# Two modulation vectors of layer 0 computed on VectorE instead of TensorE

## The chip, the cores and the metric

The kernel runs on one core of a Trainium2 chip. The metric is the device time of one execution in microseconds, and lower is better. The kernel computes in float32. TensorE multiplies matrices, VectorE (DVE) and ScalarE (ACT) and GpSimd (POOL) work elementwise, and SyncE (SP) issues the transfers from the main memory (HBM) into the on-chip memory (SBUF). Each engine runs its own instructions strictly in the order in which they stand in its stream, and waits for other engines through semaphores.

## The reference

Two blocks of two layers each, on a sequence of 256 tokens, a context of 256 tokens and a width D = 1024. The first block has a differential attention layer (layer 0, 8 heads of two 64-wide halves) and a neighbourhood attention layer, both with a feed-forward part; the second block has two hybrid layers. What the change touches is the modulation of layer 0:

```python
silu_c, silu_cc = silu(c), silu(c_ctx)          # two vectors of 1024
sh1, sc1, g1, sh2, sc2, g2 = split(silu_c @ ada_w[i] + ada_b[i], 6)   # the same with silu_cc for the context
h = rmsnorm(x, norm_mix[i]) * (1 + sc1) + sh1
y, yc = diff_attention(h, hc, ...)              # 8 heads
x = x + g1 * y
h2 = rmsnorm(x, norm_ffn[i]) * (1 + sc2) + sh2  # needed only after the attention
x = x + g2 * conv_ffn(h2, ...)
```

A vector such as sc2 has 1024 entries, held as 8 columns of 128, each for two conditionings (token and context). Each column is a product of a 1024 x 128 block of weights with two vectors.

## The kernel before, in words

A float32 product is made of three TensorE products of a high and a low part (mm3, L332, L335, L336). The weights come by DMA into a tile "raw" (128 x 2048, 1 MB, three buffers in turn for everybody), ScalarE rounds them to the high part "whi" (L311) and VectorE forms the low part "wlo" = raw - whi (L312), each in pieces of 128 x 1024.

Layer 0 starts with norms and projections of v, and then goes through eight heads. For each head, proj makes q and k (24 products of 512 columns each for q and for k), which ScalarE and VectorE turn into qhi, qlo, khi, klo (L1108, L1110, L1112) after the rotary part (L1129 to L1132, of which L1130 on POOL). diff_head then forms scores on TensorE (L1122), maxima on VectorE (L1149), exponentials on ScalarE (L1151), the difference of two softmaxes on POOL and VectorE (L1157, L1158), transposes (L1163) and the product with v (L1169). At a head's end, the output is normed: squares on ScalarE (L1174), their sum "oss" (L1176 to L1178), the scaled output "p" on VectorE (L1179), four transposes of it on TensorE (L1184, called the head's end below) and the split into ohi and olo (L1185, L1186). After heads 6 and 7 the products with wo begin, whose results are added to the residual tile xT (L883).

Modulation of layer 0 on TensorE comes in 20 "pieces" (ada_piece): each loads 1 MB of weights (L368), runs 8 products of 256 columns on a quarter of the array (L384), copies on ScalarE (L393), transposes twice on TensorE (L399) and sums on VectorE (L405, L408, and L416 for a scale). A piece gives two columns. Eight pieces (shift and scale of the attention's norm) come ahead of the attention; twelve ("fill": gate, and shift and scale of the feed-forward norm) stand in the heads, by the row (2,2,2,2,1,1,1,1) of numbers by head. Modulation of the other layers is made later on VectorE in another way (L441): a row of weights times the broadcast silu(c) "cb", summed along the row by one instruction with an accumulator (scalar_tensor_tensor), which gives one column for one conditioning; cb is loaded and put through Silu at L428 and L429.

The residual tile xT holds 8 rows of 512 columns per partition. In the attention its first two rows are scratch for q and k, and they are loaded again (L907) in head 6.

A scheduler sets the order of the instructions on each engine; buffers set when a transfer may start.

Of the kernel before, what the change touches and what calls it, by code (L numbers as in the profile page):

```python
# [11 lines left out]
AF = mybir.ActivationFunctionType  # L12
ALU = mybir.AluOpType
# [3 lines left out]
P = 128  # L17
D = 1024
KC = 8
# [6 lines left out]
NFH = NF // 2  # L26
HORD = [0, 2, 1, 3]

PIECES = [((0, k), (1, k)) for k in range(KC)] + [((2, k), (3, k)) for k in range(KC)]
PIECES += [((4, 2 * k), (4, 2 * k + 1)) for k in range(KC // 2)]  # L30
ADAV = [(0, 5, k) for k in range(KC)] + [(1, v, k) for v in (0, 1, 2, 3, 4, 5) for k in range(KC)]


# [117 lines left out]
def _layout(i):  # L151
    a = {}
# [10 lines left out]
        [np.stack([aw[0, :, :, v, k] for v, k in pc], axis=2).transpose(1, 0, 2, 3).reshape(P, KC * 256) for pc in PIECES]  # L163
    )
    a["adav"] = np.stack([aw[l, :, :, v, k].reshape(D, P).T for l, v, k in ADAV])
    a["cb"] = np.broadcast_to(c2.reshape(1, 2 * D), (P, 2 * D))
    wq = i["a_wqkv"][0]
    order = [x for h in range(8) for x in (h, 8 + h)]
# [59 lines left out]
class K:  # L228
# [191 lines left out]
    def ada_steps(self, pool, n, after):  # L420

        nc = self.nc
        if self.aq >= 2 * len(ADAV):
            return
        if self.acb[1:] != [pool]:
            cb = self.t(pool, [P, 2, D], "cb")
            nc.vector.tensor_copy(cb[:, 0, 0:1], after)
            nc.sync.dma_start(cb, self.i["cb"].rearrange("p (c k) -> p c k", c=2))  # L428
            nc.scalar.activation(cb, cb, AF.Silu)  # L429
            self.acb = [cb, pool]  # L430
        for _ in range(n):
            if self.aq >= 2 * len(ADAV):
                return
            e, c = divmod(self.aq, 2)
            self.aq += 1
            l, v, k = ADAV[e]
            if c == 0:
                self.araw = self.t(pool, [P, D], "araw", bufs=3)
                nc.sync.dma_start(self.araw, self.i["adav"][e])
            junk = self.t(pool, [P, D], "junk", mybir.dt.bfloat16)  # L440
            nc.vector.scalar_tensor_tensor(  # L441
                junk, self.araw, 1.0, self.acb[0][:, c, :], op0=ALU.mult, op1=ALU.mult,
                accum_out=self.ada[l][:, v, k, c : c + 1],
            )
            if self.aq % (2 * KC) == 0:
                self.ada_vector(e // KC)

    def ada_vector(self, g):

        nc = self.nc  # L450
        l, v, _ = ADAV[g * KC]
        ab = self.V("adab").rearrange("p (l v k) -> p l v k", l=DEPTH, v=6)[:, l, v, :]
        dst = self.ada[l][:, v, :, :]
        nc.vector.tensor_tensor(
            dst, dst, ab.rearrange("p (k o) -> p k o", o=1).to_broadcast([P, KC, 2]), op=ALU.add
        )
        if v in (1, 4):
            w = 0 if v == 1 else 1
            gn = self.V("nmix" if w == 0 else "nffn")[:, l * KC : l * KC + KC]
            nc.vector.scalar_tensor_tensor(  # L460
                self.nA[l][w], dst, 1.0, gn.rearrange("p (k o) -> p k o", o=1).to_broadcast([P, KC, 2]),
                op0=ALU.add, op1=ALU.mult,
            )
# [274 lines left out]
    def layer0(self):  # L738
        nc, i = self.nc, self.i
        with ExitStack() as cx:  # L740
# [156 lines left out]
            for h in range(8):  # L897
                q, k = nxt
                self.diff_head(hp, h, q, k, v, nlam, ohi, olo)
                if h < 7:  # L900
                    nxt = proj(h + 1)
                for _ in range((2,2,2,2,1,1,1,1)[h]):
                    self.ada_piece(fill.pop(0))
                if h == 6:
                    for hf in range(2):
                        c = slice(T * hf, T * hf + T)
                        nc.sync.dma_start(self.xT[:, 0:2, c], i["xin"][hf, :, 0:2, :])  # L907
                    wo_load(0, 1)
                    for m in (4, 5):
                        wo(0, m, (0, 1), self.acc)  # L910
# [846 lines left out]
```

## Time and profile before

| | us |
|---|---|
| runs of the kernel, median (lowest to highest of 3) | 1579.35 (1578.86 to 1582.08) |
| the profiled execution | 1579.73 |
| its span from the first to the last instruction | 1577.9 |
| TensorE (PE) busy in the span | 1548.6 (98%) |
| VectorE (DVE) busy | 1116.0 (71%) |
| ScalarE (ACT) busy | 770.1 (49%) |
| GpSimd (POOL) busy | 345.7 (22%) |
| layer-0 attention, about | 84 to 292 of the span |

Times in the profile are microseconds from the span's start. A busy share of an engine is an average: what a change is worth is read from the stretch in which it stands, and from which wait ends last there. "PEld" is TensorE's loading of weights, which runs beside its products. "PEclk" is the granted clock of TensorE as a share of full speed. A line of the code is given as L12.

### The profile page before, as it was taken

What the parts mean: (1) busy time and instruction counts of PE and PEld (TensorE: products, weight loads), DVE (VectorE), ACT (ScalarE), POOL (GpSimd) and SP (SyncE); (2) the same over time, 40 slices, a digit from 0 to 9 for tenths busy, and PEclk for the clock granted to TensorE, in tenths of its full rate; (3) what the DMA queues carried; (4) which work ended last, traced back from release to release, by engine and by line L of the source; (5) the groups of instructions that cost most, each with busy time, mean ns of one, the idle gap of its engine ahead of it and who ended that gap; (6) DMA issues with size and microseconds to landing.
All of it is one profiled execution on the core that took longest, in us unless ns stands there. A gap on an engine that the chain in (4) does not pass through costs nothing. (4 is left out here: it accounts for less than half of the span.)

```text
span 1577.9 us, 26663 instructions
## 1 busy us (share of the span) xinstructions
PE 1548.6 (98%) x10390; PEld 1354.7 (86%) x10390; DVE 1116.0 (71%) x2006; ACT 770.1 (49%) x1385; POOL 345.7 (22%) x418
## 2 busy tenths in 40 slices
PE   8999999999999999999999999999999999999998
PEld 6777777788888888888777899999899999899998
DVE  4556777678999999363554796778577667767665
ACT  4445554454322443343544684665554445555443
POOL 0012221321100111200111150123345214242222
PEclk9999999999999999999999999999999999999999
DMA  8523332335467654233221445547235555335552
GB/s 335 193 80 134 112 149 91 118 121 194 155 211 273 209 179 152 95 130 125 106 95 67 161 163 199 187 155 280 102 137 177 180 207 216 134 108 201 175 200 81
DMA packets 49373, 251.93 MB, mean 160 GB/s; under 512 B 5088, under 2 KB 8160, under 8 KB 31584
## 3 DMA queue, kind: packets, MB, share of 16 engines
q1 hardware_dynamic: 49248, 250.23, 44.4%
q8 instruction: 82, 1.34, 0.3%
q14 instruction: 43, 0.35, 0.1%
HBM read 249.16 MB, written 1.05 MB: 159 GB/s over the span
## 5 line engine op out<-in xcount | busy, mean ns | idle before, releaser
L311 ACT ACTIVATE whi<-raw 128x1024 fp32r<-128x1024 f32 (+2 forms) x372 | 372.0, 1007 | 442.8 <-PE acc L335 183.7
L312 DVE TENSOR_TENSOR wlo<-raw,whi 128x1024 fp32r<-128x1024 f32 (+2 forms) x372 | 443.6, 1196 | 165.7 <-ACT whi L311 162.2
L332 PE MATMUL acc<-hhi,whi 128*128 128x256 f32 (+1 forms) x816 | 269.4, 330 | 2.9 <-DVE nt L619 1.4
L336 PE MATMUL acc<-hhi,wlo 128*128 128x256 f32 (+1 forms) x816 | 267.5, 328 | 0.3 <-DVE wlo L312 0.3
L335 PE MATMUL acc<-hlo,whi 128*128 128x256 f32 (+1 forms) x816 | 266.6, 327 | 0.0
L332 PE MATMUL S<-hhi,whi 128*128 128x256 f32 (+1 forms) x568 | 180.7, 318 | 1.8 <-DVE u L637 1.8
L336 PE MATMUL S<-hhi,wlo 128*128 128x256 f32 (+1 forms) x568 | 180.1, 317 | 0.0
L335 PE MATMUL S<-hlo,whi 128*128 128x256 f32 (+1 forms) x568 | 179.4, 316 | 0.0
L332 PEld LDWEIGHTS acc<-hhi,whi 128*128 128x128 f32 x816 | 153.3, 188 | 23.9 <-issue 9.5
L336 PEld LDWEIGHTS acc<-hhi,wlo 128*128 128x128 f32 x816 | 153.5, 188 | 17.8 <-issue 4.2
L335 PEld LDWEIGHTS acc<-hlo,whi 128*128 128x128 f32 x816 | 153.3, 188 | 16.6 <-issue 3.8
L441 DVE SCALAR_TENSOR_TENSOR junk<-araw,cb 128x1024 bf16<-128x1024 f32 x112 | 144.6, 1291 | 2.0 <-ACT cb L429 1.5
L643 POOL TENSOR_TENSOR u<-u,u 128x256 f32<-128x256 f32 (+1 forms) x46 | 57.5, 1252 | 360.2 <-ACT u L642 356.3
L332 PEld LDWEIGHTS S<-hhi,whi 128*128 128x128 f32 x568 | 106.5, 188 | 9.2 <-ACT ghi L361 2.0
L336 PEld LDWEIGHTS S<-hhi,wlo 128*128 128x128 f32 x568 | 106.6, 188 | 8.4
L335 PEld LDWEIGHTS S<-hlo,whi 128*128 128x128 f32 x568 | 106.6, 188 | 8.0
L1490 POOL TENSOR_TENSOR macc<-macc,mm 128x256 f32<-128x256 f32 x48 | 49.2, 1024 | 162.6 <-DVE mm L1488 162.6
L332 PE MATMUL acc<-hlo,whi 128*128 128x256 f32 x288 | 81.7, 284 | 0.0
L335 PE MATMUL acc<-hhi,whi 128*128 128x256 f32 x288 | 81.5, 283 | 0.0
L336 PE MATMUL acc<-hlo,wlo 128*128 128x256 f32 x288 | 81.3, 282 | 0.0
L336 PE MATMUL S<-ghi,wlo 128*128 128x256 f32 (+1 forms) x231 | 75.7, 328 | 0.0
L332 PE MATMUL S<-ghi,whi 128*128 128x256 f32 (+1 forms) x231 | 75.6, 329 | 0.0
(436 smaller groups left out, 3575.8 us busy)
## 6 DMA issues: line engine op xcount, KB each, us to landing
raw<-in_up SPq DMA_DIRECT2D x44, 1024.0 KB, 4.8
raw<-in_mg SPq DMA_DIRECT2D x32, 1024.0 KB, 5.1
araw<-in_adav SPq DMA_DIRECT2D x56, 512.0 KB, 4.0
raw<-in_t SPq DMA_DIRECT2D x24, 1024.0 KB, 4.8
raw<-in_down SPq DMA_DIRECT2D x32, 704.0 KB, 4.1
raw<-in_ada SPq DMA_DIRECT2D x16, 1024.0 KB, 4.9
raw<-in_aqk SPq DMA_DIRECT2D x8, 1024.0 KB, 4.9
raw<-in_bqk SPq DMA_DIRECT2D x8, 1024.0 KB, 4.8
```

The lines of the kernel that those rows point to most:

```text
L311: nc.scalar.activation(hi[:, :n], raw, AF.Copy)
L312: nc.vector.tensor_tensor(lo[:, :n], raw, hi[:, :n].bitcast(F32), op=ALU.subtract)
L332: first = nc.tensor.matmul(ps, wh, x[0], start=start, stop=False)
L335: nc.tensor.matmul(ps, wh, x[1], start=False, stop=False)
L336: nc.tensor.matmul(ps, wl, x[0], start=False, stop=stop)
L441: nc.vector.scalar_tensor_tensor(junk, self.araw, 1.0, self.acb[0][:, c, :], op0=ALU.mult, op1=ALU.mult, accum_out=self.ada[l][:, v, k, c ...
L643: nc.gpsimd.tensor_tensor(us[0], us[0], us[1], op=ALU.mult)
L1490: nc.gpsimd.tensor_tensor(acc, acc, m, op=ALU.add)
```

## The change

The PE pieces of layer 0 go from 20 to 12: in the attention only the gate (v=2) is left, four pieces, one in each of heads 0 to 3. The feed-forward scale and shift (v=4 and v=3), 16 columns for two conditionings each, are made on VectorE by the new ada_first, called (2,2,1,1,1,1,0,0) times by head. Each call loads 1 MB of weights (two columns) into a raw buffer and runs four scalar_tensor_tensor over 1024 elements, two columns by two conditionings. The broadcast silu(c) lies in rows 2 to 5 of xT, and the unused product in rows 6 and 7. Since those rows are overwritten, all eight rows of the residual are loaded again in head 6, by four transfers of 512 KB instead of two of 256 KB. ada_vector, which adds the bias and forms the gain for a whole vector, takes layer and vector as its arguments.

```diff
--- before.py
+++ after.py
@@ -26,8 +26,8 @@
 NFH = NF // 2
 HORD = [0, 2, 1, 3]
 
-PIECES = [((0, k), (1, k)) for k in range(KC)] + [((2, k), (3, k)) for k in range(KC)]
-PIECES += [((4, 2 * k), (4, 2 * k + 1)) for k in range(KC // 2)]
+PIECES = [((0, k), (1, k)) for k in range(KC)] + [((2, 2 * k), (2, 2 * k + 1)) for k in range(KC // 2)]
+ADA0 = [(v, k) for v in (4, 3) for k in range(KC)]
 ADAV = [(0, 5, k) for k in range(KC)] + [(1, v, k) for v in (0, 1, 2, 3, 4, 5) for k in range(KC)]
 
 
@@ -163,6 +163,8 @@
         [np.stack([aw[0, :, :, v, k] for v, k in pc], axis=2).transpose(1, 0, 2, 3).reshape(P, KC * 256) for pc in PIECES]
     )
     a["adav"] = np.stack([aw[l, :, :, v, k].reshape(D, P).T for l, v, k in ADAV])
+    ac = [aw[0, :, :, v, k].reshape(D, P).T for v, k in ADA0]
+    a["ada0"] = np.stack([np.concatenate(ac[2 * n : 2 * n + 2], axis=1) for n in range(KC)])
     a["cb"] = np.broadcast_to(c2.reshape(1, 2 * D), (P, 2 * D))
     wq = i["a_wqkv"][0]
     order = [x for h in range(8) for x in (h, 8 + h)]
@@ -443,12 +445,34 @@
                 accum_out=self.ada[l][:, v, k, c : c + 1],
             )
             if self.aq % (2 * KC) == 0:
-                self.ada_vector(e // KC)
-
-    def ada_vector(self, g):
-
-        nc = self.nc
-        l, v, _ = ADAV[g * KC]
+                self.ada_vector(l, v)
+
+    def ada_first(self):
+
+        nc = self.nc
+        cb = self.xT[:, 2:6, :].rearrange("p a t -> p (a t)").rearrange("p (c k) -> p c k", c=2)
+        if self.af == 0:
+            nc.sync.dma_start(cb, self.i["cb"].rearrange("p (c k) -> p c k", c=2))
+            nc.scalar.activation(cb, cb, AF.Silu)
+        raw = self.t(self.st, [P, 2048], "raw", bufs=3)
+        nc.sync.dma_start(raw, self.i["ada0"][self.af])
+        junk = self.xT[:, 6:8, :].rearrange("p a t -> p (a t)")
+        for e in range(2):
+            v, k = ADA0[2 * self.af + e]
+            for c in range(2):
+                nc.vector.scalar_tensor_tensor(
+                    junk, raw[:, e * D : e * D + D], 1.0, cb[:, c, :], op0=ALU.mult, op1=ALU.mult,
+                    accum_out=self.ada[0][:, v, k, c : c + 1],
+                )
+        self.af += 1
+        if 2 * self.af % KC == 0:
+            self.ada_vector(0, v)
+
+    af = 0
+
+    def ada_vector(self, l, v):
+
+        nc = self.nc
         ab = self.V("adab").rearrange("p (l v k) -> p l v k", l=DEPTH, v=6)[:, l, v, :]
         dst = self.ada[l][:, v, :, :]
         nc.vector.tensor_tensor(
@@ -899,12 +923,15 @@
                 self.diff_head(hp, h, q, k, v, nlam, ohi, olo)
                 if h < 7:
                     nxt = proj(h + 1)
-                for _ in range((2,2,2,2,1,1,1,1)[h]):
+                for _ in range((1, 1, 1, 1, 0, 0, 0, 0)[h]):
                     self.ada_piece(fill.pop(0))
+                for _ in range((2, 2, 1, 1, 1, 1, 0, 0)[h]):
+                    self.ada_first()
                 if h == 6:
                     for hf in range(2):
                         c = slice(T * hf, T * hf + T)
-                        nc.sync.dma_start(self.xT[:, 0:2, c], i["xin"][hf, :, 0:2, :])
+                        for u in range(2):
+                            nc.sync.dma_start(self.xT[:, 4 * u : 4 * u + 4, c], i["xin"][hf, :, 4 * u : 4 * u + 4, :])
                     wo_load(0, 1)
                     for m in (4, 5):
                         wo(0, m, (0, 1), self.acc)
```

How the instructions stand is read from the built programs, in which a line of the new kernel has a number 24 to 27 higher in the attention (L1179 became L1206, L1184 became L1211). The number behind a name is that of its buffer.

VectorE at the end of head 0, before: from the first maximum of head 1's second block of scores (S_1014) to head 0's scaled output (p_856), and the row behind it.

```order
L1149 TENSOR_REDUCE nm_1013<-S_1014 128x1
L1176 TENSOR_REDUCE oss_858<-p_856 128x4
L1177 TENSOR_SCALAR oss_858<-oss_858 128x4
L1155 RECIPROCAL nm_988<-nm_988 128x2
L1156 TENSOR_TENSOR nm_988<-nm_988,nlam_584 128x1
L1179 TENSOR_TENSOR p_856<-misc_745,oss_858 128x512
L1158 SCALAR_TENSOR_TENSOR p_998<-p_998,nm_988,p_1001 128x512
```

The same place now (S_1010 is the same block of scores), as far as the sum of squares; raw_1211 is the fourth load of ada_first.

```order
L1176 TENSOR_REDUCE nm_1009<-S_1010 128x1
L463 SCALAR_TENSOR_TENSOR xT_71,ada_6_76<-raw_1211,xT_71 128x1024 x2
L1156 STREAM_SHUFFLE sw_1178<-xT_71 128x256
L463 SCALAR_TENSOR_TENSOR xT_71,ada_6_76<-raw_1211,xT_71 128x1024
L1158 TENSOR_TENSOR xT_71<-xT_71,rope_581 128x256
L1203 TENSOR_REDUCE oss_858<-p_856 128x4
L463 SCALAR_TENSOR_TENSOR xT_71,ada_6_76<-raw_1211,xT_71 128x1024
L1159 TENSOR_TENSOR xT_71<-xT_71,sw_1178 128x256
L1182 RECIPROCAL nm_984<-nm_984 128x2
L1204 TENSOR_SCALAR oss_858<-oss_858 128x4
L1176 TENSOR_REDUCE nm_1009<-S_1011 128x1
L1176 TENSOR_REDUCE nm_1043<-S_1044 128x1
```

And on to p_856.

```order
L478 TENSOR_TENSOR ada_6_76<-ada_6_76,vec_72 128x16
L1183 TENSOR_TENSOR nm_984<-nm_984,nlam_584 128x1
L1176 TENSOR_REDUCE nm_1043<-S_1045 128x1
L1137 TENSOR_TENSOR klo_1184<-xT_71,khi_1183 128x512
L484 SCALAR_TENSOR_TENSOR nA_9_79<-ada_6_76,vec_72 128x16
L1206 TENSOR_TENSOR p_856<-misc_745,oss_858 128x512
```

Four sums of 1024 elements and twelve other rows now stand between S_1010 and p_856 where four short rows stood.

TensorE ahead of the end of head 2, before: scores of head 2, two products of the projection for head 3 (acc_1638), and the end.

```order
L1122 MATMUL S_1530<-khi_1428,qhi_1393 128x256
L1122 MATMUL S_1530<-klo_1429,qhi_1393 128x256
L1122 MATMUL S_1530<-khi_1428,qlo_1394 128x256
L336 MATMUL acc_1638<-hhi_121,wlo_1600 128x512
L332 MATMUL acc_1638<-hhi_121,whi_1599 128x512
L1184 MATMUL misc_1345<-cst_69,p_1338 128x128 x4
L384 MATMUL misc_1434<-raw_1432,cs_73 32x256 x8
```

The same place now.

```order
L1149 MATMUL S_1510<-khi_1420,qlo_1386 128x256
L1149 MATMUL S_1511<-khi_1420,qhi_1385 128x256
L1149 MATMUL S_1511<-klo_1421,qhi_1385 128x256
L1149 MATMUL S_1511<-khi_1420,qlo_1386 128x256
L1211 MATMUL misc_1337<-cst_69,p_1330 128x128 x4
L386 MATMUL misc_1426<-raw_1424,cs_73 32x256 x8
L334 MATMUL acc_1812<-hhi_121,whi_1804 128x512
```

Before, products of the projection for head 3 stood in every part of the way from head 1's end to head 2's; now they stand ahead of head 1's end, and none of a projection is left between the two ends.

The queue of SP over heads 0 to 2, before: weights of the heads' q and k (aqk) and pieces (ada).

```order
L368 DMA raw_950<-in_ada 128x2048
L368 DMA raw_968<-in_ada 128x2048
L321 DMA raw_1111<-in_aqk 128x2048
L368 DMA raw_1191<-in_ada 128x2048
L368 DMA raw_1209<-in_ada 128x2048
L321 DMA raw_1352<-in_aqk 128x2048
```

And now (L370 is a piece, L458 is ada_first).

```order
L370 DMA raw_950<-in_ada 128x2048
L458 DMA raw_970<-in_ada 128x2048
L458 DMA raw_976<-in_ada 128x2048
L323 DMA raw_1107<-in_aqk 128x2048
L370 DMA raw_1187<-in_ada 128x2048
L458 DMA raw_1205<-in_ada 128x2048
L458 DMA raw_1211<-in_ada 128x2048
L323 DMA raw_1344<-in_aqk 128x2048
```

raw_1344 stands behind four loads of ada_first and takes the buffer of raw_1211.

## Rows read from the trace of the kernel before

**Rows 1.** Busy time of each engine, page of the profile.

```profile
PE 1548.6 (98%) x10390; PEld 1354.7 (86%) x10390; DVE 1116.0 (71%) x2006; ACT 770.1 (49%) x1385; POOL 345.7 (22%) x418
```

**Rows 2.** Busy time by stretch: head 0, heads 1 and 2, heads 4 to 7.

```profile
84.00:125.00 41.00, 41.00 (x202) 31.14 (x200) 22.37 (x50) 17.71 (x40) 6.41 (x9) 1.00 0.18 67
125.00:172.00 47.00, 45.78 (x292) 34.14 (x292) 32.52 (x81) 24.43 (x59) 10.39 (x14) 1.00 0.37 135
...
194.00:292.00 98.00, 94.13 (x561) 72.33 (x559) 65.92 (x157) 47.68 (x109) 17.86 (x24) 1.00 0.34 124
```

**Rows 3.** What TensorE waited for, 80 to 300: total, times, longest.

```profile
PE misc L1184 <- DVE p L1179: 3.5, 1, 3.5
...
PE acc L332 <- ACT whi L311: 0.8, 2, 0.5
```

**Rows 4.** TensorE's timeline at the end of head 0: start, duration, instruction.

```profile
125.03 0.66 PE L1184 MATMUL misc<-cst,p 128*128 128x128 f32 x4
125.61 1.93 PE L384 MATMUL misc<-raw,cs 128*32 128x256 f32 x32
127.48 0.49 PE L1122 MATMUL S<-khi,qhi 64*128 64x256 f32 x2
...
128.14 0.44 PE L399 MATMUL misc<-cst,apart 128*128 128x128 f32 x2
128.41 0.60 PE L1163 MATMUL misc<-cst,p 128*128 128x128 f32 x4
```

**Rows 5.** The accumulating sums of line 441: ns min/median/max.

```profile
L441 DVE SCALAR_TENSOR_TENSOR junk<-araw,cb x112: 1206/1214/2323, 367.5 to 629.9; 128x1024 bf16<-128x1024 f32 x112
L441 DVE DVE_READ_ACCUMULATOR junk<-araw,cb x112: 73/78/86, 368.6 to 631.0; 128x1 f32 x112
```

**Rows 6.** VectorE's timeline at the end of head 0.

```profile
119.07 0.68 DVE L1149 TENSOR_REDUCE nm<-S 128x1 f32<-128x512 f32 x1
121.53 0.69 DVE L1176 TENSOR_REDUCE oss<-p 128x4 f32<-128x512 f32 x1 [1.78 <-ACT p L1174]
122.26 0.17 DVE L1177 TENSOR_SCALAR oss<-oss 128x4 f32<-128x4 f32 x1
...
123.54 0.69 DVE L1179 TENSOR_TENSOR p<-misc,oss 128x512 f32<-128x512 f32 x1 [0.31 <-POOL oss L1178]
```

**Rows 7.** VectorE in the heads, 80 to 292, by shape: count, busy us, mean ns.

```profile
L312 DVE TENSOR_TENSOR wlo<-raw,whi 128x1024 fp32r<-128x1024 f32 x23 | 27.8, 1219 | 6.3 <-ACT whi L311 6.3
L1149 DVE TENSOR_REDUCE nm<-S 128x1 f32<-128x512 f32 x32 | 21.3, 686 | 11.2 <-PE S L1122 11.0
L1149 DVE TENSOR_REDUCE nm<-S 128x1 f32<-128x256 f32 x32 | 12.8, 418 | 5.6 <-PE S L1122 5.4
...
L1131 DVE TENSOR_TENSOR xT<-xT,rope 128x256 f32<-128x256 f32 x15 | 9.2, 610 | 0.2
L1129 DVE STREAM_SHUFFLE sw<-xT 128x256 f32<-128x256 f32 x15 | 6.6, 441 | 0.0
L1132 DVE TENSOR_TENSOR xT<-xT,sw 128x256 f32<-128x256 f32 x15 | 6.3, 422 | 3.6 <-POOL sw L1130 3.1
L1110 DVE TENSOR_TENSOR klo<-xT,khi 128x512 fp32r<-128x512 f32 x8 | 5.5, 691 | 0.5 <-ACT khi L1108 0.5
```

**Rows 8.** DMA issues in the heads: KB each, median us to landing.

```profile
raw<-in_ada SPq DMA_DIRECT2D x11, 1024.0 KB, 4.8
...
xT<-in_xin SPq DMA_DIRECT2D x2, 256.0 KB, 3.3
```

**Rows 9.** Stretches around TensorE's 3.5 us wait at head 7's end.

```profile
288.00:292.00 4.00, 0.67 (x5) 0.43 (x4) 1.54 (x4) 0.70 (x2) 1.01 (x1) 1.00 0.00 0
292.00:296.00 4.00, 3.81 (x23) 2.08 (x24) 0.79 (x2) 1.07 (x2) 0.00 (x0) 0.57 0.06 10
```

**Rows 10.** A sum of line 441 on VectorE, then the POOL row that ran beside it.

```profile
368.73 2.20 DVE L441 SCALAR_TENSOR_TENSOR junk<-araw,cb 128x1024 bf16<-128x1024 f32 x1
...
368.09 1.76 POOL L643 TENSOR_TENSOR u<-u,u 128x512 f32<-128x512 f32 x1 [7.65 <-ACT u L642]
```

## The prediction

> **What bounds the kernel now.** I read the page first: TensorE is busy for 98% of the span and VectorE for 71% [rows 1], so work taken from TensorE should be worth its full length, and VectorE seems to have room. The second view, busy time by stretch, says where: in head 0 TensorE is busy for all 41.0 us and VectorE for 22.4 of them, in heads 1 and 2 for 32.5 of 47.0, in heads 4 to 7 for 65.9 of 98.0 [rows 2]. The third view, what TensorE waits for, is nearly empty in the heads: one wait of 3.5 us for "p" at the end of head 7, and 0.8 us for whi [rows 3]. So before the change VectorE's idle time costs nothing, and its room in head 0 is 41.0 - 22.4 = 18.6 us, in heads 1 and 2 14.5 us. The question is whether the added work lies in that room where the order puts it.
>
> **What is removed.** Eight pieces. Two pieces' products take 125.61 to 127.48, 0.94 us each, and a piece's transposes 128.14 to 128.41, 0.27 us [rows 4]: 1.21 us of TensorE per piece, 9.7 us for eight. All of it stands on TensorE, which has no idle time beside it, so this is a full gain: -9.7. The copies and small sums of the pieces on ScalarE and VectorE lie beside TensorE and are counted at nothing.
>
> **What is added.** 32 accumulating sums. Such a sum takes 1.21 us and its accumulator read 0.08, and the read starts some 0.07 us before the sum's end, so 1.22 us each [rows 5]: 39 us of VectorE. The output was bfloat16 there and is float32 now; wlo, with two inputs and a 4-byte output of the same size, takes 1.22 too [rows 7], so I change nothing. 16 of the 32 (19.5 us) are ahead of head 0's p on VectorE. The room there was 18.6 us less the end of the stretch, so VectorE is full, and p cannot be in time even if every idle moment could be used.
>
> *Head 0's end.* Before, S_1014's maximum began at 119.07 and ended at 119.75, p ended at 124.23 and TensorE used it at 125.03, without a wait [rows 4, 6]; 2.5 us of that way were idle (1.78 + 0.44 + 0.31). Now these rows stand between that maximum and p: four sums (4.9), a shuffle (0.44), two rotary rows (0.61 + 0.42), the sum of squares (0.69), klo (0.69), one maximum of 512 and two of 256 columns (0.69 + 0.84) and five short rows (0.8 at the 0.17 of L1177), 10.1 us together [rows 6, 7]. Starting at 119.75, p ends at 119.75 + 10.1 + 0.69 = 130.5, and TensorE, with the same content ahead of it as before, is at its transposes at 125.03: a wait of 5.5 us. Behind the transposes stand everything of head 1 and the projection for head 2. The bounds: 3.0, if the rows behind the sums overlap as the reads do and TensorE comes 1 to 2 us later on its own; 7.0, if VectorE is 1.5 us behind at S_1010, since 12 sums (14.6 us) have nearly filled the room ahead of it. I take 5.5.
>
> At this place a rule of the Trainium skill speaks against the change: "GPSIMD Engine Reference", section "Specifications", says that GpSimd shares its SBUF interfaces with VectorE and contends with VectorE instructions that read two inputs from SBUF, as these sums do. The trace agrees: a sum of line 441 took 2.20 us where a GpSimd row ran beside it [rows 10], against 1.21. By it each of the two sums that stand behind a shuffle, while GpSimd does the rotary product, would be up to 1.0 us longer, and head 0's wait up to 7.5. I leave it out of the sum, as the GpSimd row here is 128x256 and short.
>
> *Late weights.* The load for head 2's projection (raw_1344) takes the buffer of raw_1211, whose last sum ends, by the rows above, at 119.75 + 4.9 + 0.44 + 0.61 + 0.69 = 126.4. Landing takes 4.8 us [rows 8], whi about as long as a wlo [rows 7], and then wlo another 1.22: 131.2, 132.4, 133.6, later still where VectorE has p and the next difference to do first. TensorE would reach the first product at 130.5 + 0.6 (transposes) + 0.94 (piece) + some 0.8 (transposes and one score) = 132.8, and needs wlo 0.9 us later. I take 1.8 us, between 0 and 3.0. The same chain for head 4's load (raw_1802 behind raw_1671) I take at 1.0, between 0 and 2.0.
>
> *Head 2's end.* Between the ends of heads 1 and 2 no product of a projection is left on TensorE: a piece (1.21), four transposes (0.6), 12 transposes and 12 products with v (some 3.3) and eight blocks of scores (some 5.4), 10.5 us by the steps of [rows 4]. VectorE has from olo on about 15.6 us to p, 4.9 of them sums and the rest the rows of [rows 7]. If both start together, TensorE waits 15.6 - 10.5 = 5.1 us; where VectorE's first rows are done ahead, less. Bounds 0 and 5.1; I take 3.5.
>
> *The clock.* Behind the 3.5 us wait at head 7's end TensorE was granted 0.57 of its clock for 4 us, 1.00 elsewhere [rows 9]: 4 x 0.43 = 1.7 us lost beside the wait. A wait of 5.5 us should do the same: +1.7 once, between 0 and 3.4 (if head 2's wait does it too). The Trainium skill, "TensorE: Matmul & The Clock Gate", Part 1, says that the clock has two levels and falls to half after idleness; the trace agrees with its 0.57 of mixed halves. By that rule both waits would cost it, 3.4 us.
>
> *The rest.* The cb load and its Silu come ahead of the attention, in time in which ScalarE has little to do, but ahead of a load of v's weights on the SP queue: +0.5, between 0 and 1. The reload of the residual grows from 0.5 to 2 MB, in 4 transfers for 2 of 3.3 us [rows 8]; its second half stands behind weights of the up-projection and is needed after head 7, where wo products of about 10 us cover it: 0, between 0 and 3. The head-7 wait of 3.5 us stays.
>
> Sum: -9.7 + 5.5 + 1.8 + 1.0 + 3.5 + 1.7 + 0.5 = +4.3. The profiled execution took 1579.73 us (span 1577.9), 0.4 above the median of 1579.35, so the forecast is 1579.35 + 4.3 = 1583.7, rounded to 1584.
>
> **The rivals.**
>
> *VectorE's waits are small (faster).* The heads do have 18.6 + 14.5 us of room and more behind, and a late head 0 gives VectorE and the loads time to recover before head 2. If head 0's wait is 3.0 (its lower bound) and those behind it are worth 1.0 in all, the time is 1579.35 - 9.7 + 3.0 + 1.0 + 0.5 = 1574. If there is no wait at all, it is 1570. Against it: the sums stand ahead of p in the order, and VectorE takes nothing out of order. It decides by when the transposes of head 0 start: before 128 this rival holds, after 130 mine.
>
> *The saving is just eaten (same).* Head 0 costs 5.5 + 1.7 and the loads 1.8 + 0.5, and head 2 finds VectorE ahead, because the 30 us of TensorE's work between the ends of heads 0 and 1 let it catch up: -9.7 + 9.5 = -0.2, 1579. For it: VectorE has only some 20 us in that stretch.
>
> *Everything falls due (much slower).* Upper bounds at head 0 and head 2, late weights twice and the clock twice: -9.7 + 7.0 + 3.0 + 2.0 + 5.1 + 3.4 + 1.0 = +11.8, 1591. For it: all three raw buffers are held by sums or pieces, so a late VectorE delays weights, and late weights delay scores.
>
> **How the numbers follow.** My forecast with its near surroundings (1582.5 to 1588) has 0.41, much slower 0.10, the same 0.27, faster 0.22. A measurement of this kernel can tell 0.2%, 3.2 us, from no change: slower than 1582.5 is 0.51, faster than 1576.2 0.22, between them 0.27. The range for 8 times in 10 reaches from the faster rival at 1573.5 to the much slower one at 1591; the forecast's own range is 1581 to 1588.
>
> **What would show it.** In the new profile VectorE should be nearly without idle time from 95 to 130; TensorE's list of waits should have the head's end waiting for p (L1206) with 4 to 7 us at about 125, and a second one of 2 to 5 us at head 2; a wait for whi or wlo of 1 to 3 us should follow the first; the granted clock should fall for some 4 us behind the first wait; TensorE's busy time, without clock losses, should be 9 to 10 us less. The prediction is wrong if the head's end of head 0 starts before 128, if sums last well under 1.2 us, or if the residual's reload ends up as a wait on TensorE after head 7.

## The result and the profile after

The changed kernel takes 1597.5 us (median of 4 runs, 1595.4 to 1600.5) against 1579.1 for the kernel before: ratio 1.0109, with a 95% interval of [1.0094, 1.0124], so some 17 us slower. The forecast was 1584, with 1581 to 1588 as its own range and 1573.5 to 1591 for 8 times in 10: the direction was right, the size was not.

The first line of the profile after answers to [rows 1]. TensorE is not less busy than before (1548.6), though it has 9.7 us less to do, and 12 us more of its span are idle.

```profile
PE 1552.5 (97%) x10246; PEld 1354.6 (85%) x10246; DVE 1148.9 (72%) x2049; ACT 769.1 (48%) x1378; POOL 354.3 (22%) x418
```

Busy time by stretch, for head 0, heads 1 and 2, head 3, and heads 4 to 7, answers to [rows 2]; the columns are length, PE, PEld, DVE, ACT, POOL, and the granted clock. VectorE is at 45.1 of 49.0 us in head 0, and the clock is below 1.00 in every stretch.

```profile
84.00:133.00 49.00, 43.66 (x205) 32.33 (x204) 45.13 (x91) 18.48 (x41) 9.65 (x10) 0.96 0.39 144
133.00:187.00 54.00, 47.73 (x260) 35.42 (x260) 39.15 (x90) 24.20 (x58) 12.83 (x14) 0.94 0.32 117
187.00:224.00 37.00, 36.52 (x185) 27.22 (x185) 32.41 (x70) 17.22 (x36) 10.20 (x10) 0.95 0.49 176
224.00:313.00 89.00, 82.81 (x423) 62.63 (x421) 55.16 (x128) 40.69 (x97) 15.54 (x22) 0.92 0.23 82
```

What TensorE waited for from 80 to 340 (total, times, longest) answers to [rows 3].

```profile
PE misc L1211 <- DVE p L1206: 7.9, 3, 3.6
PE S L1149 <- ACT p L1178: 4.4, 4, 1.4
PE misc L1190 <- DVE p L1185: 2.0, 2, 1.8
PE acc L334 <- ACT whi L313: 1.7, 2, 1.3
PE misc L1196 <- ACT aT L1191: 1.7, 4, 0.5
```

*Head 0.* TensorE's timeline answers to [rows 4]: behind the last product with v (L1196) stand only nine score products (L1149), and TensorE is idle for 0.30 us ahead of that product and for 1.42 and 3.57 us behind it. The piece behind it (L386) then takes twice its time: the clock is at half.

```profile
125.16 0.71 PE L1196 MATMUL misc<-v,aT 128*128 128x128 f32 x4 [0.30 <-ACT aT L1191]
127.29 0.49 PE L1149 MATMUL S<-khi,qhi 64*128 64x512 f32 x1 [1.42 <-ACT p L1178]
132.91 1.09 PE L1211 MATMUL misc<-cst,p 128*128 128x128 f32 x4 [3.57 <-DVE p L1206]
...
133.93 1.94 PE L386 MATMUL misc<-raw,cs 128*32 128x256 f32 x16
```

VectorE's timeline of the same stretch answers to [rows 6]; it has no idle time from 120.8 on, the four sums (L463) are ahead of p, and p ends at 132.8.

```profile
120.81 1.89 DVE L1176 TENSOR_REDUCE nm<-S 128x1 f32<-128x512 f32 x3 [0.42 <-PE S L1149]
122.61 1.22 DVE L463 SCALAR_TENSOR_TENSOR xT<-raw,xT 128x1024 f32<-128x1024 f32 x1
...
127.96 1.21 DVE L463 SCALAR_TENSOR_TENSOR xT<-raw,xT 128x1024 f32<-128x1024 f32 x1
...
132.09 0.68 DVE L1206 TENSOR_TENSOR p<-misc,oss 128x512 f32<-128x512 f32 x1
```

A sum takes 1219 ns in the median (the row gives minimum, median and maximum), close to the 1214 of [rows 5].

```profile
L463 DVE SCALAR_TENSOR_TENSOR xT<-raw,xT x32: 1197/1219/1768, 86.6 to 214.7; 128x1024 f32<-128x1024 f32 x32
```

*Head 2.* Waits again, in several pieces of 0.5 to 1.8 us, most of them ahead of the head's last product with v; for p itself (L1211, the last row) TensorE does not wait:

```profile
179.63 0.71 PE L1196 MATMUL misc<-v,aT 128*128 128x128 f32 x4 [0.47 <-ACT aT L1191]
182.11 0.41 PE L1190 MATMUL misc<-cst,p 128*128 128x128 f32 x2 [1.77 <-DVE p L1185]
182.99 0.71 PE L1196 MATMUL misc<-v,aT 128*128 128x128 f32 x4 [0.47 <-ACT aT L1191]
185.06 0.79 PE L1149 MATMUL S<-khi,qhi 64*128 64x512 f32 x1 [1.36 <-ACT p L1178]
187.33 1.11 PE L1211 MATMUL misc<-cst,p 128*128 128x128 f32 x4
```

*Heads 6 and 7.* These stretches of 4 us answer to [rows 9]. From 292 to 320 the clock is at half most of the time, also from 296 to 304, where TensorE shows no idle time at all. The last sum was at 214.7, so no sum of VectorE is near.

```profile
288.00:292.00 4.00, 2.17 (x14) 1.55 (x13) 1.22 (x5) 2.75 (x7) 0.76 (x1) 1.00 0.00 0
292.00:296.00 4.00, 3.14 (x15) 2.30 (x14) 3.00 (x6) 1.40 (x5) 0.93 (x2) 0.61 0.00 0
296.00:300.00 4.00, 4.00 (x10) 2.28 (x10) 2.26 (x8) 2.16 (x9) 1.17 (x2) 0.50 0.00 0
300.00:304.00 4.00, 4.00 (x11) 3.10 (x11) 1.23 (x4) 0.57 (x2) 0.48 (x1) 0.50 0.00 0
304.00:308.00 4.00, 4.00 (x25) 3.70 (x25) 0.00 (x0) 0.98 (x2) 0.00 (x0) 0.69 0.00 0
308.00:312.00 4.00, 1.51 (x12) 1.12 (x9) 0.89 (x3) 1.09 (x3) 0.82 (x1) 1.00 0.00 0
312.00:316.00 4.00, 2.17 (x7) 1.61 (x8) 1.44 (x2) 0.69 (x1) 0.18 (x1) 0.67 0.02 4
316.00:320.00 4.00, 4.00 (x14) 3.33 (x14) 2.78 (x6) 2.36 (x6) 0.00 (x0) 0.50 0.00 0
```

**An account of the span.** Read in steps of 1 us, the view by stretch gives for each step TensorE's idle time (1 less its busy time) and its clock loss (busy time times 1 less the granted clock). What is left of the span is work at full clock.

| us | before | after | change |
|---|---|---|---|
| work at full clock | 1543.4 | 1534.7 | -8.7 |
| idle | 28.4 | 40.5 | +12.1 |
| clock loss | 6.1 | 18.6 | +12.5 |
| span | 1577.9 | 1593.7 | +15.8 |

Nearly all of both changes lies between 60 and 400. The account of each experiment below is of that part of one execution, and it is rough: e2, e5 and e9 below run the same TensorE instructions, and their work over the whole span comes out as 1537.8, 1529.9 and 1536.8 us; and up to 60, where e2, e5, e8, e9 and e12 are not edited, their clock loss is 3.3, 1.7, 6.6, 3.0 and 3.2 us. Differences of a few us in one of its columns therefore say little.

**Bare ends.** The order of TensorE's instructions tells where the idle time is. Between a head's last product with v and the transposes of p at its end lies a chain of squares, sum, power and scaled output on the other engines (L1201 to L1206). I call an end bare if TensorE has there nothing but the nine score products of the next head, or nothing. Before, one end is bare (head 7's); the others have 13 to 31 products of a projection or of wo there. After, four are bare: heads 0, 2, 6 and 7. Those are the four heads at which the trace shows the large waits, 5.3, 4.3, 2.6 and 3.5 us; at head 2, where no product of a projection is left between the ends of heads 1 and 2, 2.9 of the 4.3 us stand ahead of the last product with v.

### The profile page after: what moved, and what is told of

Its sections match the earlier page's. It is cut to its first block, busy times and chain, and to the rows that moved or that the text cites. A ratio compares the mean times of both kernels' runs of the same rounds, so it can differ in the third digit from the quotient of the medians.

```text
span 1593.7 us, 26437 instructions
## 1 busy us (share of the span) xinstructions
PE 1552.5 (97%) x10246; PEld 1354.6 (85%) x10246; DVE 1148.9 (72%) x2049; ACT 769.1 (48%) x1378; POOL 354.3 (22%) x418
## 5 line engine op out<-in xcount | busy, mean ns | idle before, releaser
L1517 POOL TENSOR_TENSOR macc<-macc,mm 128x256 f32<-128x256 f32 x48 | 49.1, 1024 | 162.7 <-DVE mm L1515 162.7
```

Of the source, the lines that this page charges most:

```text
L1517: nc.gpsimd.tensor_tensor(acc, acc, m, op=ALU.add)
```

## The experiments

Ratios are to runs of the kernel before on the same chip; the last columns are of the profiled execution, from 60 to 400.

| run | median us | ratio, 95% interval | idle us | clock loss us | bare ends |
|---|---|---|---|---|---|
| before | 1579.1 | | 8.0 | 3.4 | 7 |
| after | 1597.5 | 1.0109 [1.0094, 1.0124] | 21.2 | 15.5 | 0, 2, 6, 7 |
| e1_short | 1584.5 | 1.0045 [1.0021, 1.0069] | 11.3 | 17.1 | 6, 7 |
| e2_nopieces | 1589.1 | 1.0074 [1.0053, 1.0095] | 13.1 | 11.2 | 5, 6, 7 |
| e3_behind | 1611.1 | 1.0223 [1.0197, 1.0249] | 30.2 | 24.3 | 0, 1, 5, 7 |
| e4_reload | 1579.5 | 1.0012 [0.9990, 1.0035] | 7.8 | 1.7 | 7 |
| e5_nphold | 1583.6 | 1.0043 [1.0027, 1.0058] | 15.1 | 11.7 | 4, 5, 6, 7 |
| e6_hold | 1600.7 | 1.0136 [1.0105, 1.0167] | 22.1 | 19.7 | 0, 2, 5, 6, 7 |
| e7_sphold | 1598.1 | 1.0137 [1.0113, 1.0161] | 21.0 | 19.9 | 1, 4, 5, 6, 7 |
| e8_npdummy | 1596.4 | 1.0126 [1.0108, 1.0144] | 14.7 | 11.7 | 5, 6, 7 |
| e9_npfill | 1580.1 | 1.0000 [0.9990, 1.0010] | 8.8 | 9.6 | none |
| e10_fill | 1596.6 | 1.0113 [1.0096, 1.0130] | 19.1 | 13.4 | 0, 2 |
| e11_beforefill | 1577.3 | 0.9982 [0.9972, 0.9992] | 5.2 | 3.4 | none |
| e12_npdummy2 | 1583.0 | 1.0018 [1.0006, 1.0031] | 7.8 | 2.5 | (filled) |
| e13_idlework | 1593.9 | 1.0080 [1.0052, 1.0107] | 10.7 | 3.3 | 1 |
| e14_both | 1613.4 | 1.0200 [1.0174, 1.0226] | 24.5 | 18.2 | 1, 7 (4: six big products) |

**The sums, the pieces, the order on VectorE and the reload, one edit at a time.** e1 shortens the sums:

```diff
-                    junk, raw[:, e * D : e * D + D], 1.0, cb[:, c, :], op0=...
+                    junk[:, 0:32], raw[:, e * D : e * D + 32], 1.0, cb[:, c, 0:32], op0=...
```

> The changed kernel, with each sum over the first 32 elements instead of 1024 (so the feed-forward shift and scale are not the reference's); loads, reload and pieces as changed. Two theories. Theory A, two causes: VectorE's sums ahead of p make TensorE wait at the ends of heads 0 and 2, and apart from them the last two heads have lost their filler (9 and 15 products with wo stand there instead of 31 and 44 and two pieces), which costs some 3 us of waits and 8 us of half clock. Then the waits at heads 0 and 2 go, idle TensorE from 120 to 200 falls from 10 us to below 3, the half clock around 290 to 320 stays for over 10 us, and the time is about 1579.1 - 9.7 + 11 = 1580.5 (1577 to 1584). Theory B, the sums cause all of it, the late heads included: about 1569.5 (1567 to 1573). Theory C, the loads in the raw buffers cause it: the waits stay, 1590 or more.

The waits at heads 0 and 2 went, and the half clock at the end stayed, with 17.1 us of loss: theory A's signs, with a time just outside its range (1584.5 against 1577 to 1584) and outside those of B and C. In the order that came out, the ends of heads 0 and 2 have 33 and 27 big products again, so the run takes away the length of the sums and the bare ends of heads 0 and 2 together. By the ratios, the two are worth some 10 us of the change's 17.

e2 takes the pieces out of the kernel before and adds nothing:

```diff
-PIECES = [((0, k), (1, k)) for k in range(KC)] + [((2, k), (3, k)) for k in range(KC)]
-PIECES += [((4, 2 * k), (4, 2 * k + 1)) for k in range(KC // 2)]
+PIECES = [((0, k), (1, k)) for k in range(KC)] + [((2, 2 * k), (2, 2 * k + 1)) for k in range(KC // 2)]
...
+            nc.gpsimd.memset(self.ada[0][:, 3:5], 0.0)
+            nc.gpsimd.memset(self.nA[0][1], 1.0)
...
-                for _ in range((2,2,2,2,1,1,1,1)[h]):
+                for _ in range((1,1,1,1,0,0,0,0)[h]):
```

> The kernel before with the eight pieces left out and nothing in their place (feed-forward shift and scale are set to constants, so the output is not the reference's). TensorE has 9.7 us less to do. Theory A: the products with wo move ahead of heads 6 and 7 here too (6 and 15 products are left there), so the waits and the half clock at the end appear with no sum and no added load: 1579 to 1582, with over 10 us of half clock from 280 to 320. Theory B: nothing is in the way, 1569.4 (1567 to 1573).

TensorE has 9.7 us less to do, nothing is added but the constants, and the kernel is 11.7 us slower (1.0074). Theory B falls; theory A had the signs right and the size too small. The profiled execution was the fastest of the four, 7.1 us over before's; in it idle time is 5.1 and clock loss 7.8 us more, so with 9.7 us less work some 4 us are left that the account does not explain. TensorE's timeline has the changed kernel's waits, at the ends of heads 6 and 7, without any sum:

```profile
279.64 0.49 PE L1123 MATMUL S<-khi,qhi 64*128 64x512 f32 x1 [1.36 <-ACT p L1152]
282.41 0.63 PE L1185 MATMUL misc<-cst,p 128*128 128x128 f32 x4 [0.81 <-DVE p L1180]
...
300.92 1.08 PE L1185 MATMUL misc<-cst,p 128*128 128x128 f32 x4 [3.52 <-DVE p L1180]
```

With the pieces gone, projections and products with wo stand further forward in TensorE's order, and the late heads are left bare.

e3 puts an edge into VectorE's order:

```diff
+                    with self.tc.issue_after(self.end):        # self.end: this head's p
                         self.ada_first()
```

> The changed kernel with one edge in VectorE's order: the sums of a head stand behind that head's scaled output p. In the order that comes out, 43 and 56 products with wo stand in heads 6 and 7. Theory A: no wait of over 2 us for p at heads 0 and 2, and a last stretch like before's: 1571 to 1578. Theory B: the same 39 us of VectorE in the heads, so waits elsewhere: 1585 or more. Theory C: loads wait longer for their buffers since the sums come later: waits for whi and wlo of over 6 us together, 1580 or more.

1611 us: theory B, and C by its time, though the waits for whi and wlo stay under its 6 us (5.4). The waits went elsewhere, for khi (5.9 us), whi (5.4), p of the heads' end (5.3) and the softmax's p (4.7), and the clock loss is the largest of all. But the order that came out also has bare ends at heads 0, 1, 5 and 7, so the run does not tell the sums from the missing filler. This move of the sums by hand does not make them fit.

e4 loads all of the residual again in the kernel before, by the four transfers of the change's last hunk:

> The kernel before, with all eight rows of the residual loaded again in head 6 (four transfers of 512 KB instead of two of 256 KB), nothing else; the order of TensorE stays. Theories A and B: covered, 1579 (1576 to 1582). Theory D, the reload delays weights or the products with wo in the last heads: 1584 or more.

No difference (1.0012 [0.9990, 1.0035]): theory D falls.

**Keeping the filler for late heads.** e5, e6 and e7 put an edge from a head's end to a group of products with wo. e5 does it without pieces and sums, e6 in the changed kernel, e7 with the calls (1,1,1,1,1,1,2,0) besides:

```diff
+                    with self.tc.issue_after(self.ends[3]):      # 4, 5, 6 for the next groups
                         for m in (4, 5):
                             wo(0, m, (0, 1), self.acc)
```

> The kernel before without the eight pieces and without sums, as in the run without pieces (feed-forward shift and scale are constants), and with edges in TensorE's order that keep the first half's products with wo for heads 4 to 7: 24, 24, 24 and 51 of them stand between the heads' ends, where it were 77 (with the last projection), 25, 6 and 15. TensorE's work is the same. Theory A (a head without big products leaves TensorE waiting and its clock at half): idle time and clock loss from 60 to 400 fall from 13.1 and 11.2 us to about 9 and 4, and the time from 1589 to about 1574 (1570 to 1578), at last below before. Rival E (what made the kernel without pieces slow has nothing to do with the filler): 1586 or more.

> The changed kernel with the same edges: 24, 24 and 51 products with wo stand in heads 5, 6 and 7 where it were 20 with the projection, 9 and 15. The order up to head 3 stays as it is. Theory A: heads 0 and 2 keep their waits of 9 to 10 us and 4 us of clock loss, the last heads lose theirs (some 3 us of idle time, some 7 us of clock): about 1587 (1583 to 1590). Theory B, VectorE's sums cause all of it: 1595 or more.

> The changed kernel with the same edges and ada_first called (1,1,1,1,1,1,2,0) times by head instead of (2,2,1,1,1,1,0,0). Theory A: in head 0 eight sums fewer stand ahead of p, so its wait falls from 5.3 us to below 1; the last heads have their filler: about 1575 (1570 to 1582), a version as fast as before or faster. Theory B (39 us more of VectorE cost what they cost wherever they stand): 1587 or more.

All three miss what theory A had, and e6 and e7 lie where theory B had them (1595 and 1587 or more). The products did stand in the late heads, but TensorE took them at each head's start, and the ends were bare as before: e7 even has five bare ends, and its waits are at heads 1, 4, 5, 6 and 7. That moved theory A from "how many big products a head has" to "whether they stand in its last stretch" (A2). e5 comes out a little faster than e2, with intervals that just overlap, and in the account by its work alone, not by idle time or clock.

e8 gives TensorE idle work in the kernel without pieces, written into the tile of the transposes at the heads' ends:

```diff
+        for _ in range({5: 8, 6: 12, 7: 12}.get(h, 0)):
+            nc.tensor.matmul(tp, k[0][:, 0:P], q[0], start=True, stop=True)
```

> The run without pieces and sums again (feed-forward shift and scale are constants), with idle work for TensorE: 8, 12 and 12 products of 128 x 512 whose result is thrown away, ahead of the transposes at the ends of heads 5, 6 and 7, 7.4 us of added work at 0.23 us each; the order stays otherwise as it was. Theory A's clock part: the waits there (2.2, 2.5 and 3.5 us) are filled, the clock stays up, the clock loss from 60 to 400 falls from 11.2 to below 5 us, and with 7 us of idle time turned into work the time falls by 5 to 8 us, to about 1582, though TensorE has more to do. Rival F (the low clock costs nothing that matters, the end is set by the waits alone): 1589 or more, by up to 7 us.

A miss that says little of the clock: the idle work ran ahead of the last product with v instead of behind it, filled none of the waits, and the kernel became slower than e2 by about the length of the added work (1596.4 - 1589.1 = 7.3 us by the medians, 8 by the ratios, for 7.4).

**Filling the last stretch.** e9 and e10 make the edge start at the last product with v of heads 4 to 7 (without pieces, and in the changed kernel); e11 does it in the kernel before for head 7 alone:

```diff
+                    with self.tc.issue_after(self.avs[7]):       # head 7's last product with v
                         for m in (0, 1):
                             wo(0, m, (0, 1), self.acc)
```

> The kernel without the eight pieces and without sums again (feed-forward shift and scale are constants), with other edges than in the run before: the products with wo may start only behind the last product with v of heads 4, 5, 6 and 7, so that 24, 24, 24 and 33 of them stand between that product and the transposes of p at the head's end, where there were only nine score products or none. Theory A2 (what counts is not how many big products a head has, but whether they stand in this last stretch, in which TensorE waits some 6 us for squares, sum, power and scaled output): no waits at the ends of heads 4 to 7, head 7's 3.5 us gone too, clock loss from 60 to 400 below 4 us, and 1566 (1562 to 1572), faster than before by its 9.7 us and 3 more. Rival E (filler does not matter, something else slows the kernel without pieces): 1582 or more.

> The changed kernel with these edges; its order up to head 3 is as it was, so heads 0 and 2 still have nine score products alone at their ends. Theory A2: the waits at the ends of heads 6 and 7 and the half clock from 292 to 320 go, some 7 us of idle time and 9 us of clock, those of heads 0 and 2 stay: 1582 (1577 to 1587). Rival E, or theory B (the sums): 1595 or more.

> The kernel before, with one edge: the last 24 products with wo of the first half (m = 0, 1) stand behind head 7's last product with v, where TensorE waited 3.5 us. Pieces as before, no sums. Theory A2: the wait and one stretch of half clock (1.7 us) go, 1579 - 5 = about 1573 (1570 to 1577). Rival E: 1577 to 1580, no difference.

e11 is faster than before, 0.9982 [0.9972, 0.9992]: 24 products with wo now stand where TensorE waited 3.5 us, and the transposes follow without a wait. Its clock loss stayed (3.4 us at another place, 273 to 281), so the gain is 3 us and not 5: just outside theory A2's range, and by the median inside rival E's, but the interval of the ratio lies below 1.

```profile
283.79 0.48 PE L332 MATMUL acc<-ohi,whi 128*128 128x512 f32 x1
...
291.20 0.39 PE L336 MATMUL acc<-ohi,wlo 128*128 128x512 f32 x1
291.43 0.60 PE L1191 MATMUL misc<-cst,p 128*128 128x128 f32 x4
```

e9 gained some 9 us on e2 (12 by the ratios), as the waits at the ends went, which rules out rival E; but it reached only the time of before and not A2's 1566. Waits of 0.3 to 1.6 us came up behind the filler (for p of the scores and the softmax), and the clock fell at them and in the thin parts of heads 4 to 6 (loss 9.6 us). e10 gained nothing on the changed kernel and lies where theory B and rival E had it: the ends of heads 6 and 7 are filled and idle time is 2 us less, but the 2 us of clock that it saves from 60 to 400 it loses again before 60, and the account puts 3 us more into work. For A2 both miss: filling the ends helps without the sums, but the filler is then missing elsewhere in these heads, and with the sums filling the late ends alone bought nothing.

**The clock by itself.** e12 is e8 with the idle work behind the last product with v (10, 10 and 14 products), e13 is the same in the changed kernel, at its four bare ends (16, 14, 10 and 14 products; the lines are those of e12):

```diff
+        with self.tc.issue_after(self.avs[-1]):
+            for _ in range({5: 10, 6: 10, 7: 14}.get(h, 0)):
+                nc.tensor.matmul(tp, k[0][:, 0:P], q[0], start=True, stop=True)
```

> The run without pieces and sums (feed-forward shift and scale are constants) with idle work again, now where TensorE waits: 10, 10 and 14 products of 128 x 512, thrown away, behind the last product with v of heads 5, 6 and 7. They add 7.8 us of work in some 7 us of waits, so without the clock nothing is to be gained: rival F says 1588 to 1591. Theory A2's clock part: TensorE's clock stays up there, the loss of 11.2 us from 60 to 400 falls below 4, and the time to about 1580 (1576 to 1584).

The stretches of e2 (first) and e12 at heads 6 and 7: with ten thrown-away products, which took 2.56 us from 282.24 on, the clock stays at 1.00.

```profile
282.00:286.00 4.00, 3.23 (x13) 2.25 (x13) 2.50 (x7) 2.76 (x8) 0.70 (x1) 0.69 0.00 0
286.00:290.00 4.00, 4.00 (x10) 2.70 (x10) 1.77 (x6) 0.59 (x3) 0.48 (x1) 0.50 0.00 0
290.00:294.00 4.00, 4.00 (x14) 3.18 (x13) 0.81 (x3) 0.54 (x2) 0.48 (x1) 0.53 0.00 0
```

```profile
282.00:286.00 4.00, 4.00 (x25) 3.06 (x23) 2.02 (x6) 2.60 (x7) 1.69 (x2) 1.00 0.00 0
286.00:290.00 4.00, 3.22 (x21) 2.42 (x21) 3.51 (x11) 2.86 (x8) 0.69 (x1) 1.00 0.00 0
290.00:294.00 4.00, 4.00 (x28) 3.54 (x27) 1.95 (x6) 1.82 (x6) 0.96 (x2) 1.00 0.00 0
```

The clock loss fell from 11.2 to 2.5 us, and the kernel became 6 us faster by the medians with 7.8 us more to do. The added work took the place of 5.3 us of idle time, so the gain is the clock's. Rival F falls: the clock is a cost of its own, beside the waits.

> The changed kernel itself with idle work for TensorE behind the last product with v: 16, 14, 10 and 14 products of 128 x 512, thrown away, at the ends of heads 0, 2, 6 and 7, 12.4 us of added work where it waited 5, 4, 3 and 4 us. In the order that comes out, head 1's end has become bare (nine score products and two others). Theory A2's clock part: the loss to the half clock from 60 to 400 falls from 15.5 us to about 6, and the time to 1590 (1584 to 1594) though TensorE has more to do. Rival F (the clock follows the waits, and only the waits cost): the added work fills the waits and no more, 1597 or more.

In the changed kernel itself the loss fell from 15.5 to 3.3 us and idle time from 21.2 to 10.7; the time fell to 1593.9, at the edge of theory A2's range. The 12.4 us of idle work take back more than half of the 22.7, and in the profiled execution another 6.5 us of idle time and clock loss come up behind 400 and 1.9 us of clock loss before 60, which no run here explains. The intervals of the two ratios overlap, so the time alone does not show a gain; the granted clock does.

**The sums with TensorE's pieces kept.**

```diff
+                    accum_out=self.adx[:, v - 3, k, c : c + 1],   # columns that nothing reads; all pieces stay
```

> The kernel before with all its pieces, and VectorE's sums, their loads and the full reload besides (the sums go into columns that nothing reads, so the output is the reference's from the pieces). TensorE's work is that of before. In the order that comes out, the ends of heads 1 and 7 are bare, head 0 has 22 big products there. Theory A2: with TensorE's own work kept as filler the sums cost one bare end, some 3 us of idle time and 3 us of clock, and some late weights: 1586 (1582 to 1590). Theory B (39 us of sums on VectorE cost what they cost): as much as lay between the run with short sums and the changed kernel, 13 us, so 1592 or more.

A clear miss of theory A2, and beyond what theory B counted (13 us): 1613.4, 32 us over before by the ratio. What TensorE waited for, from 80 to 360:

```profile
PE misc L1211 <- DVE p L1206: 8.7, 3, 3.6
PE misc L1190 <- DVE p L1185: 6.0, 4, 2.4
PE acc L335 <- ACT whi L314: 3.5, 4, 1.3
PE S L1149 <- ACT khi L1135: 3.1, 2, 2.6
```

With 39 us of sums and eight more loads in the heads, TensorE waits for p, for the softmax, for khi and for whi: idle time from 60 to 400 is 16.5 us more and clock loss 14.8 us more than before. At head 4 it waits 3.6 us for p although six big products stand there. So TensorE's own filler does not make the sums harmless. Whether VectorE's time or the loads weigh more in this run was not separated. Taking the pieces' 9.7 us off this cost would give 22 us for the change, which has 17; the orders differ, so the two do not add up exactly.

## Why the prediction was wrong

- **What is removed** (-9.7): the account has -8.7 of work, which agrees as far as the account can tell. What the prediction did not ask is what else the removal moves: in e2 it alone made the kernel slower.
- **Head 0's end** (+5.5): 0.30 + 1.42 + 3.57 = 5.3 us of idle time. The rows on VectorE took about what they were forecast to take, and a sum 1.22 us as taken, but the first of the four sums began at 122.6 and not at 119.75, so p ended at 132.8 and not at 130.5. TensorE was late too, with 1.7 us of waits for the softmax ahead of it and without the 13 products of the projection that stood there before, so its wait for p is 3.57 us, under the 4 to 7 named as the sign. That the sum of the waits agrees is in part luck. The rule weighed there (the Trainium skill, "GPSIMD Engine Reference", "Specifications") shows in the longest sum, 1.77 us, which ran beside a rotary row of GpSimd. Two other sums beside such a rotary row of GpSimd took 1.20 and 1.22 us, so leaving it out of the length of the sums was right.
- **Late weights** (+1.8 and +1.0): for the load of raw_1344, which was issued at 129.21, TensorE did not wait. The 1.25 + 0.52 us of waits for whi and wlo at 155 to 157 are for the next load of q and k weights, issued at 149.78, right behind the end of a sum of ada_first (148.53 + 1.22); 0.48 us follow at 190.8. The mechanism was right, the load was another, and the sum of 2.3 us against 2.8 is near.
- **Head 2's end** (+3.5): 0.19 + 0.47 + 1.77 + 0.47 + 1.36 = 4.3 us. From olo (171.9) to the end of p (187.1) VectorE took 15.2 us, forecast 15.6. The waits stand in the softmax ahead of the end and not at p.
- **The rest** (cb +0.5, reload 0, head 7's wait as before): idle time and clock loss up to 60 are as before (6.5 and 3.0 us against 6.6 and 2.8); e4 shows the reload to be covered; head 7's wait is 3.52 us again. But heads 6 and 7 are not as before: 0.47 + 1.36 + 0.81 us of new waits, and 0.78 behind head 7. The prediction put the late heads at nothing without counting their products; the count in the last stretch of the new order would have shown the bare end of head 6.
- **The clock** (+1.7, bounds 0 and 3.4): this step failed. The account has +12.5. In idle time the forecast's terms sum to 12.3 us and the trace has 12.1. For the places that were priced this is right (11.8 us forecast, 11.8 in the trace); for the total it is luck, since the new waits of heads 6 and 7 (3.5 us, put at nothing) are offset by smaller waits of before that went. The clock was not priced right: I charged one fall of 1.7 us to the longest wait. The clock fell at head 0 (half from 129 to 135.8), at head 2, where no single wait was over 1.8 us (183.6 to 190.4), at head 6, with waits of 0.5 to 1.4 us (292.8 to 306.5), at head 7 (313.3 to 320.1) and once near 342. The rule weighed there (the Trainium skill, "TensorE: Matmul & The Clock Gate", Part 1), read as "each wait costs it", was nearer than my sum, and still short by the late heads. [Rows 9] were read as if the clock fell nowhere else; the trace of before has a second fall, of 1.7 us, near 320, behind two waits of 1.2 and 1.1 us (two rows of TensorE's timeline, and the stretch from 319 to 323 with its granted clock of 0.59):

```profile
316.56 0.39 PE L332 MATMUL acc<-hhi,whi 128*128 128x256 f32 x1 [1.17 <-ACT hhi L545]
318.03 0.58 PE L512 MATMUL misc<-cst,naccc 128*128 128x2 f32 x4 [1.08 <-DVE naccc L481]
...
319.00:323.00 4.00, 4.00 (x23) 4.00 (x22) 3.38 (x11) 1.42 (x3) 0.94 (x1) 0.59 0.06 25
```

Had the clock been taken at each of the four bare ends, with the loss that the trace of after has there (1.6, 2.7, 6.5 and 3.0 us), the sum would have been -9.7 + 12.3 + 13.8 less the 1.6 of before's head 7: +14.8, or 1594. That uses losses that only the trace of after shows. At 1.7 us for each of the three new bare ends, all that the trace of before could tell, it would have been -9.7 + 12.3 + 5.1 = +7.7, or 1587.

What stays open: why filling the late ends in e10 gave nothing, for which the account is too rough; and why the half clock at head 6 lasted 13.7 us. A version in which VectorE's sums are free was not found: every run with the sums at full length took some 1594 us or more. e11 is the one that beats both kernels, and it has no sums.

## What to carry to other kernels

Here, taking work from a TensorE that is 98% busy did not pay, because the work that was left no longer stood at its waits. For a change of this kind count, in the order of the changed kernel, the big products in each stretch in which TensorE waits for a chain of the other engines, and price each bare stretch with its wait and with the half clock behind it, which here cost as much as the waits (12.5 against 12.1 us). Work moved to an engine that is 70% busy on average is not in its idle time if it stands ahead of what TensorE waits for: the sums alone, with TensorE's own work kept, cost 32 us (e14). And a wait is filled by putting work behind the last instruction that starts its chain, not by giving the head more work (e5 to e8 against e9, e11 and e12).

## What the runs showed of the hardware

The granted clock stayed at half for 13.7 us from 292.8 on in the changed kernel, although TensorE shows no idle time from 294 to 308. From 297.6 to 304.6 TensorE ran 13 products of 128 x 512 and three score products there (two of the 13 are shown), so neither busy time in the trace nor products of this size brought the clock back within that stretch. Why it stayed low so long is open.

```profile
297.67 0.79 PE L337 MATMUL acc<-olo,whi 128*128 128x512 f32 x1
...
303.34 0.63 PE L334 MATMUL S<-ohi,whi 128*128 128x512 f32 x1
```

The clock also fell at head 2 behind waits of 0.5 to 1.8 us each, which no single long wait explains. Products of 128 x 512 that fill the wait before the clock falls did hold it: with ten of them at head 6 it stayed at 1.00 in e12, where e2, the same kernel without them, had it at half from 283.5 to 293.8. At head 5 of e12 ten such products did not prevent a later fall, from 268.8 to 275.6, amid other waits.

Rows of GpSimd were longer beside VectorE's sums. The softmax row L1184 of 128 x 256 took 0.48 us at 180.01, and 1.36, 1.89 and 1.54 us at 148.7, 176.0 and 196.7, where a sum of VectorE lay beside most of it; the sums there kept their 1.21 to 1.22 us. Durations on GpSimd are rough.

```profile
175.99 1.89 POOL L1184 TENSOR_SCALAR p<-p,nm 128x256 f32<-128x256 f32 x1 [3.40 <-ACT p L1178]
176.32 1.21 DVE L463 SCALAR_TENSOR_TENSOR xT<-raw,xT 128x1024 f32<-128x1024 f32 x1
...
180.01 0.48 POOL L1184 TENSOR_SCALAR p<-p,nm 128x256 f32<-128x256 f32 x1 [2.13 <-DVE nm L1183]
```
